# GpSimd's subtractions on VectorE, and a margin behind the data for background matmuls

## Chip, cores and metric

The kernel runs on one core of a Trainium2 chip. The metric is the device time of one execution in microseconds; before the change three runs gave a median of 1106.71 (1105.04 to 1108.61).

## What is computed

Two request groups of 512 positions by 1024 channels go through the same two encoder layers and a final norm, in float32:

```python
def encoder_layer(x, c, g_norm, w_ada, b_ada, w_in, w_out, decay_fwd, decay_bwd):
    ...
    mod = jax.nn.silu(c) @ w_ada + b_ada
    shift, scale, gate = jnp.split(mod, 3, axis=-1)
    h = rmsnorm(x, g_norm) * (1.0 + scale[:, None, :]) + shift[:, None, :]
    proj = h @ w_in
    qa, ka, va, ga, qb, kb, vb, gb = jnp.split(proj, idx, axis=-1)
    ...
    ya = oa.reshape(B, S, A_WIDTH) * jax.nn.silu(ga)
    ...
    r = yf + yb
    r = r * lax.rsqrt(jnp.mean(r * r, axis=-1, keepdims=True) + EPS)
    yr = r.astype(x.dtype).reshape(B, S, R_WIDTH) * jax.nn.silu(gb)
    out = jnp.concatenate([ya, yr], axis=-1) @ w_out
    return x + gate[:, None, :] * out
```

Mixer A is window attention with rotary query and key in three dilations, merged by their softmax denominators; mixer B is retention in both directions with a norm for each head.

## The kernel before

**High and low halves.** Float32 products are made of three matmuls on rounded operands: high by high, high by low and low by high. The high half is a rounding copy (ScalarE), the low half the difference between the value and its high half. So each operand costs one conversion and one subtraction. The input weights come in 56 tiles of 128x1024 (`raw`, made into `wH` and `wL` by `prepper`, line 797), the output weights in 16 (`rawo` into two `wo`, `prep_o`, line 830). The hidden state of layer 0 comes in eight tiles of 128x512 for each input (`hT`, `first_affine`, line 728), the mixed outputs as `yT` (`splitter`, line 1182). GpSimd does three of the subtractions: all `wL`, the second `wo`, and the low `hT` of the second input in layer 0. VectorE does the rest.

**Stages.** For each layer the kernel walks through a list of items: projections of query and key pairs of the window attention ("p"), of retention ("r"), their values ("v", "w") and gates ("g"), each for input 0 and then input 1. An item of one weight tile is 24 matmuls for each input. Rotary tables, attention scores, softmax, transposes by DMA, value products, retention products and norms of the items that are done run as background work between the matmuls of later items. After the items comes the output projection (`wo` by `yT`), then the residual and the norm of the next layer. At the start the modulation products (`wa` by `siluT`) come in pieces as their weights land; the projection matmuls of the first items for input 0 lie between them, and then the second input's hidden tiles are made: a transpose on TensorE, a copy and a conversion on ScalarE, a scaling on VectorE (`xT`) and the subtraction.

**The retention norm.** `r_out` (line 1135) adds up the squares of four heads on TensorE (four matmuls 32x512 by `small`), takes the inverse root on VectorE in place (`rsqrt`, line 484: two integer operations and three rounds of three), writes the rows `nwr` and broadcasts them with four matmuls by `selg`. It happens twice in a layer.

**What sets the order.** The instructions are written out by a planner while the program is built. `Plan` (line 128 on) keeps a planned time at which each engine is free and each tile is ready; `note` moves it on by a table of costs for each operation. Background steps are generators that yield a condition, the planned time from which they may be issued. Before each main matmul `pump` (line 220) issues every background step whose time is not behind TensorE's planned time; where the main matmul itself isn't ready, it issues the earliest one. Once written, the order is fixed; on the chip an instruction starts when its semaphores allow it. Two functions give the times: `at` (the tiles' planned time plus LAT, 200 ns) for steps that go to TensorE or to a transfer, and `after(engine, ...)` for steps of another engine, which is zero as soon as the tiles are ready before that engine is free. For VectorE and GpSimd the planner also keeps a list of times at which one holds the other off (`port`, `held`).

All engine calls go through one helper, so every row of the profile names line 391; the tiles tell what it is.

Of the kernel before, what the change touches and what calls it, by code (L numbers as in the profile page):

```python
# [47 lines left out]
AHEAD = 3000.0  # L48
LAT = 200.0
SAME = {"DVE": 127.0}  # L50
NMAIN = 5
# [73 lines left out]
class Plan:  # L125


    def __init__(self):
        self.free = {"PE": 0.0, "DVE": 0.0, "ACT": 0.0, "POOL": 0.0, "SP": 0.0}
        self.dma = 0.0  # L130
        self.port = {"DVE": [], "POOL": []}
        self.ready = {}
        self.last = {}
        self.slots = {}
        self.dead = set()
        self.tasks = []

    def keys(self, a):
# [21 lines left out]
    def held(self, eng, start, cost):  # L160

        other = self.port["POOL" if eng == "DVE" else "DVE"]
        for s, e in other:
            if s < start + cost and e > start:
                start = e
        own = self.port[eng]
        own.append((start, start + cost))
        del own[:-64]
        return start

    def note(self, eng, cost, outs, ins, nbytes=0.0, port=False):
# [209 lines left out]
class Engine:  # L381
# [5 lines left out]
    def __getattr__(self, op):  # L387
        fn = getattr(self.eng, op)

        def call(*args, **kw):  # L390
# [10 lines left out]
            if self.name == "SP":  # L401
                nbytes = outs[0].free_size() * outs[0].shape[0] * (2.0 / 290.0 if outs[0].dtype == F16 else 4.0 / 360.0)
            psum = any(a.tensor.name.startswith("banks") for a in ins)
            port = self.name == "POOL" or (self.name == "DVE" and not psum)
            self.plan.note(self.name, self.cost(op, outs, ins), outs, ins, nbytes, port)
            return r
        return call

    def cost(self, op, outs, ins):
# [26 lines left out]
        if self.name == "POOL":  # L436
            return 30.0 + 2.37 * n
        if op == "dma_start_transpose":
# [5 lines left out]
def trunk_kernel(  # L444
# [8 lines left out]
    plan = Plan()  # L453
    V, A, G, T, Q = (Engine(plan, n, e) for n, e in (("DVE", nc.vector), ("ACT", nc.scalar), ("POOL", nc.gpsimd),
                                                     ("PE", nc.tensor), ("SP", nc.sync)))
    cp = ctx.enter_context(tc.tile_pool(name="cp", bufs=1))
# [131 lines left out]
    def first_mod(ks):  # L588
        nk = len(ks)
        yield lambda: H.avail(2, 2 * nk, 8)  # L590
        w = first_load(ks)
        yield lambda: max(plan.at(bias, siluT, *w[0:2]), B.avail())
        bk = B.take()
# [7 lines left out]
        for k in range(KT):  # L601
            if k == 4 and nk == 2:
                yield lambda: plan.at(*w[2:4])
            for n in range(2 * nk):
# [8 lines left out]
        B.free(bk)  # L613
        yield lambda: max(plan.at(m), B.avail())
        cb = B.take()
# [112 lines left out]
    def first_affine(b, k, bk, xT):  # L728
# [3 lines left out]
        else:  # L732
            A.activation(xT, bk, AF.Copy)
        B.free(bk)
        yield lambda: (max(plan.after("ACT", xT), plan.after("DVE", xT), plan.at(acol, scol), H.avail(1, 2, 4, "R"))
                       if ("cols", 0, k) in have else INF)
# [11 lines left out]
    def prep_h(l, b):  # L748
        keys = [(l, b, t) for t in range(TT)]
        for k in range(KT):  # L750
            yield lambda: (max(plan.at(*(xh[x] for x in keys)), plan.at(acol, scol), B.avail(), H.avail(1, 2, hold[0], "R", 1))
                           if ("cols", l) in have and all(x in xh for x in keys) else INF)
# [44 lines left out]
    def prepper():  # L797
        for job in jobs:
            wts[job] = []
            for t in range(ntiles(*job[1:])):  # L800
# [29 lines left out]
    def prep_o(l):  # L830
        for k in KORDER:
# [26 lines left out]
    def main_wide(pj, job, l, b):  # L858
        for t in range(TT):
            out = pj[:, t // 2, (t % 2) * 256:(t % 2) * 256 + 256]  # L860
            for k in range(KT):
                pump(lambda: (max(plan.at(*wts[job][k // 4][2:]), plan.at(*hT[(l, b, k)]))
                              if (l, b, k) in hT and len(wts.get(job, ())) > k // 4 else INF))
# [8 lines left out]
    def rope(pj, c, s, res, b):  # L872
# [18 lines left out]
        for i, x in enumerate((*hi, *lo)):  # L891
            yield lambda: plan.at(x) - 700.0
            Q.dma_start(rd[:, i % 2, i // 2, :], x)
        H.free(*c, *s)
        yield lambda: max(plan.at(rd) - 500.0, H.avail(1, 6, K_STK, "R"))
        out = []
# [63 lines left out]
    def soften(p, b, ih, h, sS, tn, res):  # L960
# [22 lines left out]
        for t in pts[1:]:  # L983
            yield lambda: max(plan.at(t), W_T.avail())
            pT = W_T.take(1, "pT")
# [56 lines left out]
    def value(p, pj, res):  # L1042
# [13 lines left out]
        B_IN.free(pj)  # L1056
        yield lambda: max(plan.at(vt), W_T.avail())
        vn = W_T.take(1, "vn")
# [188 lines left out]
    def store(dst, src):  # L1247
        yield lambda: plan.at(src)
        Q.dma_start(split(dst, 2), src)
# [27 lines left out]
    for l in range(DEPTH):  # L1277
# [77 lines left out]
        for b in range(NB):  # L1355
            for t in range(TT):
# [8 lines left out]
                for c, (n0, n1) in enumerate(LAST if final else ((0, D),)):  # L1365
                    for n, k in enumerate(KORDER):
                        pump(lambda: plan.at(*yT[(k, b)], *wo[k]) if (k, b) in yT and k in wo else INF)
                        y, w = ([x.bitcast(F32R) for x in z] for z in (yT[(k, b)], wo[k]))
# [48 lines left out]
```

## Time and profile before

| | before |
|---|---|
| median of three runs | 1106.71 us |
| the profiled execution | 1106.17 us |
| its span, first to last instruction | 1104.0 us |
| TensorE busy | 1052.3 us |
| VectorE busy | 774.1 us |
| ScalarE busy | 467.8 us |
| GpSimd busy | 194.7 us |
| mean granted clock of TensorE | 0.987 |

TensorE's busy time covers a matmul until its modelled end, so what can be read from it is mainly where it has none. The granted clock (PEclk) is 1.00 at 2.4 GHz and 0.50 at 1.2 GHz; a stretch with 0.91 spent part of its time at the lower level. An idle time in brackets behind a row stands in front of that instruction, and the name behind the arrow is what ended it.

### The profile page before, as it was taken

To read this page: it belongs to the slowest core of one execution; us is meant where nothing else is said; L and a number is where in the kernel's file an instruction comes from. 1 tells how busy PE (TensorE), PEld (TensorE's weight loads), DVE (VectorE), ACT (ScalarE), POOL (GpSimd) and SP (SyncE) were. 2 spreads that over 40 slices of the span, in tenths; PEclk is the share of its full clock that TensorE was granted. 3 is DMA by queue.
4 is the path that set the end of the run, shared out by engine and by line. 5 is a ranking of instruction groups with operands and counts; after the bars stand their busy time and mean duration, and the time that the engine had idled before them with its cause. 6 is when DMAs were issued, how large, how long until landed. Compare 5 with 4: busy or idle time off the path is not lost.

```text
span 1104.0 us, 14884 instructions
## 1 busy us (share of the span) xinstructions
PE 1052.3 (95%) x5443; PEld 832.7 (75%) x5443; DVE 774.1 (70%) x1536; ACT 467.8 (42%) x808; POOL 194.7 (18%) x84
## 2 busy tenths in 40 slices
PE   5989999989999899989999999989999899999997
PEld 3758578877688777767888778867798777778886
DVE  5686655598565988767447885589766987757555
ACT  6455413418234266572233552426434257534101
POOL 3152010120101111181000111112101111143000
PEclk9989999999999999989999999999999999999999
DMA  9826995069970599964221697048851599942232
GB/s 314 310 64 185 272 311 180 5 231 233 299 245 20 173 227 268 219 163 152 77 86 68 229 182 237 20 134 205 188 165 44 186 227 263 211 115 96 77 115 77
DMA packets 217337, 189.64 MB, mean 172 GB/s; under 512 B 156656, under 2 KB 167184, under 8 KB 217264
## 3 DMA queue, kind: packets, MB, share of 16 engines
q1 hardware_dynamic: 217264, 188.69, 60.5%
q8 instruction: 43, 0.70, 0.3%
q14 instruction: 30, 0.25, 0.1%
HBM read 117.34 MB, written 33.57 MB: 137 GB/s over the span
## 4 chain that ended last, share of the span: by engine, by line
PE 73%; DVE 13%; DMA 3%; SPq 2%; issue 2%; ACT 1%; POOL 1%; DVEq 0%; POOLq 0%; ACTq 0%
PE banks L391 73%; DVE yr L391 2%; DVE rsq L391 2%; SPq L391 2%; DVE th L391 1%; DVE hT L391 1%; DVE sd L391 1%; DMA KL<-stk_dram 1%; DVE pt L391 1%; DVE rc L391 1%; DMA wa<-in_w_ada_dram 1%; DVE xT L391 1%; DMA pT<-pt 1%; DMA raw<-in_w_in_dram 0%; DMA KS<-stk_dram 0%
## 5 line engine op out<-in xcount | busy, mean ns | idle before, releaser
L391 PE MATMUL banks<-hT,wH 128*128 128x512 f32 x1536 | 484.0, 396 | 6.7 <-POOL hT L391 4.4
L391 PEld LDWEIGHTS banks<-hT,wH 128*128 128x128 f32 x1536 | 288.4, 190 | 83.7 <-issue 14.8
L391 PE MATMUL banks<-hT,wL 128*128 128x512 f32 x768 | 301.3, 392 | 0.0
L391 POOL TENSOR_TENSOR wL<-raw,wH 128x1024 fp32r<-128x1024 f32 x56 | 141.2, 2529 | 724.6 <-ACT wH L391 635.1
L391 PE MATMUL banks<-wo,yT 128*128 128x512 f32 (+1 forms) x792 | 179.5, 388 | 5.1 <-DVE yT L391 2.8
L391 PEld LDWEIGHTS banks<-wo,yT 128*128 128x128 f32 x792 | 146.5, 190 | 36.6 <-DVE yT L391 4.9
L391 PEld LDWEIGHTS banks<-hT,wL 128*128 128x128 f32 x768 | 145.6, 190 | 30.8
L391 PE MATMUL banks<-wH,hT 128*128 128x256 f32 x512 | 97.3, 284 | 0.0
L391 PEld LDWEIGHTS banks<-wH,hT 128*128 128x128 f32 x512 | 81.7, 191 | 4.0 <-issue 2.5
L391 ACT ACTIVATE wH<-raw 128x1024 fp32r<-128x1024 f32 x56 | 58.2, 1052 | 42.4 <-DMA raw<-in_w_in_dram 30.6
L391 PE MATMUL banks<-wL,hT 128*128 128x256 f32 x256 | 72.4, 283 | 0.0
L391 ACT ACTIVATE sq<-xr 128x1024 bf16<-128x1024 f32 (+2 forms) x18 | 17.3, 963 | 114.8 <-DVE xr L391 71.0
L391 DVE SCALAR_TENSOR_TENSOR pt<-sS,sm,pt 128x512 f16<-128x512 f32 x65 | 60.9, 977 | 3.4 <-ACT pt L391 2.8
L391 ACT ACTIVATE sS<-sS,sm 128x512 f32<-128x512 f32 x65 | 46.2, 712 | 28.8 <-DVE sm L391 28.0
L391 DVE TENSOR_TENSOR res<-banks,gb 128x512 f32<-128x512 f32 (+1 forms) x33 | 22.1, 671 | 49.0 <-PE banks L391 49.0
L391 DVE CUSTOM_DVE_ANT_0 sS<-banks,tabs 128x512 f32<-128x512 f32 x65 | 42.3, 687 | 19.7 <-PE banks L391 19.6
L391 POOL TENSOR_TENSOR wo<-rawo,wo 128x1024 fp32r<-128x1024 f32 x16 | 41.2, 2595 | 49.2 <-ACT wo L391 25.4
L391 PEld LDWEIGHTS banks<-wL,hT 128*128 128x128 f32 x256 | 49.0, 191 | 1.0
L391 PE MATMUL banks<-sr,rv 128*128 128x512 f32 x169 | 47.0, 391 | 0.0
L391 PE MATMUL banks<-pT,vn 128*64 128x512 f16 x384 | 45.1, 381 | 1.3 <-DMA pT<-pt 1.3
L391 ACT ACTIVATE pt<-sS,sm 128x512 f16<-128x512 f32 x65 | 43.2, 710 | 5.6 <-DVE sm L391 3.3
L391 PE MATMUL banks<-wa,siluT 128*32 128x128 f32 (+1 forms) x384 | 33.8, 398 | 7.9 <-DMA wa<-in_w_ada_dram 7.9
(278 smaller groups left out, 1407.6 us busy)
## 6 DMA issues: line engine op xcount, KB each, us to landing
raw<-in_w_in_dram SPq DMA_DIRECT2D x56, 512.0 KB, 5.4
wa<-in_w_ada_dram SPq DMA_DIRECT2D x48, 512.0 KB, 6.6
QS<-stk_dram SPq DMA_DIRECT2D x48, 256.0 KB, 3.6
KS<-stk_dram SPq DMA_DIRECT2D x48, 256.0 KB, 4.5
KL<-stk_dram SPq DMA_DIRECT2D x44, 256.0 KB, 4.6
rawo<-in_w_out_dram SPq DMA_DIRECT2D x16, 512.0 KB, 4.6
stk_dram<-rs SPq DMA_DIRECT2D x28, 256.0 KB, 2.7
stk_dram<-sd SPq DMA_DIRECT2D x23, 256.0 KB, 2.5
```

The costliest lines, as they stand in the source:

```text
L391: r = fn(*args, **kw)
```

## The change

The subtractions of `wL`, `wo` and `hT` go to VectorE; GpSimd has no work left. In `prepper` and `prep_o` the subtraction becomes a step of its own that is issued when the high half is ready by the plan. The list of mutual holds and GpSimd's costs leave the planner. `at` no longer adds 200 ns for all tiles; it adds an amount by the engine that makes the tile (SLACK). A new function `soon` keeps the old 200 ns, and main matmuls, transfers and `after` use it; `at` stays with the background steps that go to TensorE: scores, value products, retention products, norms, modulation products and the transposes of hidden tiles.

```diff
+SLACK = {"PE": 200.0, "ACT": 400.0, "DVE": 900.0, "DMA": 1500.0}
...
+    def made(self, *tiles):
+        return [self.ready[k] for t in tiles for k in self.keys(t) if k in self.ready]
+
     def at(self, *tiles):
-        return max((self.ready.get(k, (0.0, ""))[0] for t in tiles for k in self.keys(t)), default=0.0) + LAT
+
+        return max((t + SLACK[eng] for t, eng in self.made(*tiles)), default=0.0)
+
+    def soon(self, *tiles):
+        return max((t for t, _ in self.made(*tiles)), default=0.0) + LAT
 
     def after(self, eng, *tiles):
-        t = self.at(*tiles)
+        t = self.soon(*tiles)
         return 0.0 if t <= self.free[eng] else t
...
-        if port:
-            start = self.held(eng, start, cost)
...
-        (V if b == 0 else G).tensor_tensor(h[1].bitcast(F32R), xT, h[0], op=ALU.subtract)
+        V.tensor_tensor(h[1].bitcast(F32R), xT, h[0], op=ALU.subtract)
...
-                G.tensor_tensor(lo, raw, h.bitcast(F32), op=ALU.subtract)
+                yield lambda: plan.after("DVE", w[0])
+                V.tensor_tensor(lo, raw, h.bitcast(F32), op=ALU.subtract)
...
-                    G.tensor_tensor(t.bitcast(F32R), raw, out[0], op=ALU.subtract)
+                    yield lambda: plan.after("DVE", out[0])
+                    V.tensor_tensor(t.bitcast(F32R), raw, out[0], op=ALU.subtract)
...
     def main_half(out, job, t, l, b, ks=range(KT)):
         for k in ks:
-            pump(lambda: (max(plan.at(wts[job][t][2], wts[job][t][3]), plan.at(*hT[(l, b, k)]))
+            pump(lambda: (plan.soon(*wts[job][t][2:], *hT[(l, b, k)])
```

The order of the instructions moves nearly everywhere, since each issue time depends on those before. Three places, all on VectorE, show what the prediction speaks of.

The second input's hidden tiles in layer 0, from the last step of the decays (`ldec`) on; `xT` (once `th`) is scaled in place, and `hT` is its low half. Before:

```order
L391 TENSOR_SCALAR ldec<-ldec 128x8
L391 TENSOR_SCALAR xT<-xT,acol,scol 128x512 x3
L391 SCALAR_TENSOR_TENSOR th<-th,banks 128x512
L391 TENSOR_SCALAR xT<-xT,acol,scol 128x512
L391 TENSOR_SCALAR th<-th,acol,scol 128x512
L391 TENSOR_SCALAR xT<-xT,acol,scol 128x512
L391 TENSOR_TENSOR xT<-banks,tabs 128x512
```

Now:

```order
L385 TENSOR_SCALAR ldec<-ldec 128x8
L385 TENSOR_SCALAR xT<-xT,acol,scol 128x512
L385 TENSOR_TENSOR hT<-xT,hT 128x512
L385 TENSOR_SCALAR xT<-xT,acol,scol 128x512
L385 TENSOR_TENSOR hT<-xT,hT 128x512
L385 TENSOR_SCALAR xT<-xT,acol,scol 128x512
L385 TENSOR_TENSOR hT<-xT,hT 128x512
```

Each scaling is now followed by its subtraction, eight pairs in all, and the first rotary product (`banks,tabs`) comes behind the last of them, where it came before the last two scalings.

The first retention norm, around the copy of the sums of squares out of PSUM (`TENSOR_SCALAR ...<-banks`) that begins the chain to `nwr`. Before:

```order
L391 TENSOR_TENSOR sd<-sd,rs 128x512
L391 TENSOR_SCALAR rsq<-banks 128x512
L391 TENSOR_TENSOR rsq<-rsq,rs 128x512
L391 TENSOR_TENSOR sd<-sd,rs 128x512
L391 TENSOR_SCALAR yr<-rsq 128x512
L391 TENSOR_SCALAR yr<-yr 128x512
L391 TENSOR_TENSOR yr<-yr 128x512
```

Now:

```order
L385 TENSOR_TENSOR sr<-rs,KL 128x512
L385 TENSOR_TENSOR wL<-raw,wH 128x1024
L385 TENSOR_SCALAR yr<-banks 128x512
L385 TENSOR_SCALAR nw_1989<-yr 128x512
L385 TENSOR_SCALAR sS<-nw_1989 128x512
L385 TENSOR_TENSOR nw_1989<-sS 128x512
```

A wL subtraction now stands in front of the copy, and the two rotary operations that stood between the copy and the integer operations are gone from there. On TensorE 57 projection matmuls stand between the sums and the broadcast of `nwr` before, at all four norms; now it is 51, 54, 51 and, at the last, 69 with 4 background matmuls among them.

The end of layer 0, where the output projection's operands are made; `wo` are output weights, `yT` the low halves of the mixed outputs. Before:

```order
L391 TENSOR_TENSOR y<-y,yr 128x512
L391 SCALAR_TENSOR_TENSOR yr<-yr,banks 128x512
L391 TENSOR_TENSOR sd<-sd,yr 128x512
L391 SCALAR_TENSOR_TENSOR yr<-yr,banks 128x512
L391 TENSOR_TENSOR yr<-yr 128x512
L391 TENSOR_TENSOR yT<-th,yT 128x512
L391 TENSOR_TENSOR yT<-sS,yT 128x512
```

Now:

```order
L385 TENSOR_TENSOR th<-th,yr 128x512
L385 TENSOR_TENSOR wo<-rawo,wo 128x1024 x3
L385 TENSOR_TENSOR yT<-th,yT 128x512 x2
L385 TENSOR_TENSOR yT<-yr,yT 128x512
L385 TENSOR_TENSOR yT<-th,yT 128x512
L385 TENSOR_TENSOR yT<-yr,yT 128x512
L385 SCALAR_TENSOR_TENSOR th<-th,banks 128x512
L385 TENSOR_TENSOR yT<-th,yT 128x512
```

Five `yT` now stand ahead of the last gate's product (`th<-th,banks`), which all of them followed before, and three `wo` stand ahead of them. On ScalarE six conversions to `yT` stand ahead of the last gate's tanh, where all sixteen stood behind it. On TensorE the last value product of layer 0 (24 matmuls of `pT` by `vn`) stood 9 matmuls ahead of the output projection and now stands behind its first 30.

## Rows read from the trace of the kernel before

**Rows 1.** The page: busy us, share of the span, instructions by engine.
```profile
PE 1052.3 (95%) x5443; PEld 832.7 (75%) x5443; DVE 774.1 (70%) x1536; ACT 467.8 (42%) x808; POOL 194.7 (18%) x84
```

**Rows 2.** Busy time by stretch; columns as in the first line below.
```profile
core 0: us, PE busy (x) PEld busy (x) DVE busy (x) ACT busy (x) POOL busy (x), PEclk, DMA share, GB/s
60.00:80.00 20.00, 15.56 (x69) 10.95 (x68) 17.74 (x40) 12.41 (x21) 12.67 (x9) 0.90 0.14 51
80.00:100.00 20.00, 20.00 (x82) 15.90 (x82) 9.23 (x26) 9.30 (x22) 4.34 (x2) 0.93 0.59 187
...
120.00:140.00 20.00, 18.58 (x102) 10.12 (x94) 15.72 (x40) 11.88 (x25) 0.00 (x0) 1.00 1.05 289
220.00:240.00 20.00, 16.77 (x67) 13.10 (x66) 19.49 (x26) 4.15 (x6) 5.09 (x2) 0.91 0.60 196
360.00:380.00 20.00, 17.05 (x76) 13.77 (x75) 19.52 (x26) 3.42 (x5) 5.24 (x2) 1.00 0.60 196
480.00:500.00 20.00, 15.49 (x64) 9.60 (x62) 14.03 (x8) 13.40 (x21) 20.00 (x8) 0.83 0.44 159
720.00:760.00 40.00, 37.06 (x159) 28.97 (x158) 36.06 (x68) 16.48 (x32) 5.97 (x3) 0.96 0.50 163
860.00:880.00 20.00, 16.82 (x74) 13.28 (x73) 19.59 (x35) 3.72 (x9) 1.05 (x1) 1.00 0.47 158
920.00:940.00 20.00, 18.29 (x84) 13.41 (x83) 14.01 (x40) 14.56 (x29) 2.38 (x1) 0.91 1.11 261
1020.00:1040.00 20.00, 20.00 (x90) 16.57 (x89) 10.86 (x30) 2.30 (x4) 0.00 (x0) 1.00 0.23 80
```

**Rows 3.** Timeline at the first norm: start us, us, engine, operation; VectorE, GpSimd, TensorE.
```profile
220.18 0.69 DVE L391 TENSOR_SCALAR rsq<-banks 128x512 f32<-128x512 f32 x1
...
221.99 0.42 DVE L391 TENSOR_SCALAR yr<-rsq 128x512 int32<-128x512 int32 x1
222.44 2.50 DVE L391 TENSOR_SCALAR yr<-yr 128x512 int32<-128x512 int32 x1
...
226.43 0.69 DVE L391 SCALAR_TENSOR_TENSOR yr<-yr 128x512 f32<-128x512 f32 x1
...
228.61 2.82 DVE L391 SCALAR_TENSOR_TENSOR yr<-yr 128x512 f32<-128x512 f32 x1
...
234.50 0.75 DVE L391 SCALAR_TENSOR_TENSOR nwr<-nwr,small,rsq 128x512 fp32r<-128x512 f32 x1
...
221.96 2.70 POOL L391 TENSOR_TENSOR wL<-raw,wH 128x1024 fp32r<-128x1024 f32 x1 [21.49 <-ACT wH L391]
228.49 2.39 POOL L391 TENSOR_TENSOR wL<-raw,wH 128x1024 fp32r<-128x1024 f32 x1 [3.83 <-ACT wH L391]
...
235.30 0.96 PE L391 MATMUL banks<-nwr,selg 128*128 128x512 f32 x3 [2.99 <-DVE nwr L391]
```

**Rows 4.** Timeline where the second input's hidden tiles are made: TensorE, VectorE, GpSimd.
```profile
57.78 0.50 PE L391 MATMUL banks<-hT,wH 128*128 128x512 f32 x1 [0.55 <-DVE hT L391]
...
58.35 1.94 PE L391 MATMUL banks<-small,x 128*128 128x128 f32 x16
...
77.28 0.80 PE L391 MATMUL banks<-hT,wH 128*128 128x512 f32 x1 [2.96 <-POOL hT L391]
...
80.69 1.05 PE L391 MATMUL banks<-hT,wH 128*128 128x512 f32 x2
...
57.64 0.54 DVE L391 TENSOR_SCALAR xT<-xT,acol,scol 128x512 f32<-128x512 f32 x1
...
64.18 2.43 DVE L391 TENSOR_SCALAR xT<-xT,acol,scol 128x512 f32<-128x512 f32 x3
...
64.87 5.77 POOL L391 TENSOR_TENSOR hT<-xT,hT 128x512 fp32r<-128x512 f32 x4 [33.81 <-DVE xT L391]
```

**Rows 5.** Timeline at the end of layer 0, VectorE: a first and a later yT.
```profile
489.31 2.86 DVE L391 TENSOR_TENSOR yT<-th,yT 128x512 fp32r<-128x512 f32 x1
...
500.48 0.68 DVE L391 TENSOR_TENSOR yT<-yr,yT 128x512 fp32r<-128x512 f32 x1
```

**Rows 6.** Groups of instructions: count, busy us, mean ns, idle before.
```profile
L391 DVE TENSOR_TENSOR rv<-banks,rv 128x1024 fp32r<-128x1024 f32 x8 | 9.8, 1225 | 42.0 <-ACT rv L391 42.0
```

More of the change, by code (lines that the diff above doesn't have):

```diff
@@ L128, in __init__ @@
     def __init__(self):
-        self.free = {"PE": 0.0, "DVE": 0.0, "ACT": 0.0, "POOL": 0.0, "SP": 0.0}
+        self.free = {"PE": 0.0, "DVE": 0.0, "ACT": 0.0, "SP": 0.0}
         self.dma = 0.0
-        self.port = {"DVE": [], "POOL": []}
         self.ready = {}
@@ L151, in keys, with note @@
         return [slot + (u,) for u in sorted(units)]
+    def made(self, *tiles):
+        return [self.ready[k] for t in tiles for k in self.keys(t) if k in self.ready]
     def at(self, *tiles):
-        return max((self.ready.get(k, (0.0, ""))[0] for t in tiles for k in self.keys(t)), default=0.0) + LAT
+        return max((t + SLACK[eng] for t, eng in self.made(*tiles)), default=0.0)
+    def soon(self, *tiles):
+        return max((t for t, _ in self.made(*tiles)), default=0.0) + LAT
     def after(self, eng, *tiles):
-        t = self.at(*tiles)
+        t = self.soon(*tiles)
         return 0.0 if t <= self.free[eng] else t
[L160 to L171, printed above, removed]
+    def note(self, eng, cost, outs, ins, nbytes=0.0):
         part = eng == "SP" and (outs[0].shape[0] < P or outs[0].tensor.name.startswith("stk"))
@@ L402, in call @@
                 nbytes = outs[0].free_size() * outs[0].shape[0] * (2.0 / 290.0 if outs[0].dtype == F16 else 4.0 / 360.0)
-            psum = any(a.tensor.name.startswith("banks") for a in ins)
-            port = self.name == "POOL" or (self.name == "DVE" and not psum)
-            self.plan.note(self.name, self.cost(op, outs, ins), outs, ins, nbytes, port)
+            self.plan.note(self.name, self.cost(op, outs, ins), outs, ins, nbytes)
             return r
@@ L435, in cost @@
             return (53.0 if psum else 93.0) + 93.0 * extra + 0.833 * n
-        if self.name == "POOL":
-            return 30.0 + 2.37 * n
         if op == "dma_start_transpose":
@@ L453, in trunk_kernel @@
     plan = Plan()
-    V, A, G, T, Q = (Engine(plan, n, e) for n, e in (("DVE", nc.vector), ("ACT", nc.scalar), ("POOL", nc.gpsimd),
-                                                     ("PE", nc.tensor), ("SP", nc.sync)))
+    V, A, T, Q = (Engine(plan, n, e) for n, e in (("DVE", nc.vector), ("ACT", nc.scalar), ("PE", nc.tensor),
+                                                  ("SP", nc.sync)))
     cp = ctx.enter_context(tc.tile_pool(name="cp", bufs=1))
@@ L591, in first_mod @@
         w = first_load(ks)
-        yield lambda: max(plan.at(bias, siluT, *w[0:2]), B.avail())
+        yield lambda: max(plan.soon(bias, siluT, *w[0:2]), B.avail())
         bk = B.take()
@@ L602, in first_mod @@
             if k == 4 and nk == 2:
-                yield lambda: plan.at(*w[2:4])
+                yield lambda: plan.soon(*w[2:4])
             for n in range(2 * nk):
@@ L613, in first_mod @@
         B.free(bk)
-        yield lambda: max(plan.at(m), B.avail())
+        yield lambda: max(plan.soon(m), B.avail())
         cb = B.take()
@@ L734, in first_affine @@
         B.free(bk)
-        yield lambda: (max(plan.after("ACT", xT), plan.after("DVE", xT), plan.at(acol, scol), H.avail(1, 2, 4, "R"))
+        yield lambda: (max(plan.after("ACT", xT), plan.after("DVE", xT), plan.soon(acol, scol), H.avail(1, 2, 4, "R"))
                        if ("cols", 0, k) in have else INF)
@@ L750, in prep_h @@
         for k in range(KT):
-            yield lambda: (max(plan.at(*(xh[x] for x in keys)), plan.at(acol, scol), B.avail(), H.avail(1, 2, hold[0], "R", 1))
+            yield lambda: (max(plan.at(*(xh[x] for x in keys)), plan.soon(acol, scol), B.avail(), H.avail(1, 2, hold[0], "R", 1))
                            if ("cols", l) in have and all(x in xh for x in keys) else INF)
@@ L861, in main_wide @@
             for k in range(KT):
-                pump(lambda: (max(plan.at(*wts[job][k // 4][2:]), plan.at(*hT[(l, b, k)]))
+                pump(lambda: (plan.soon(*wts[job][k // 4][2:], *hT[(l, b, k)])
                               if (l, b, k) in hT and len(wts.get(job, ())) > k // 4 else INF))
@@ L891, in rope @@
         for i, x in enumerate((*hi, *lo)):
-            yield lambda: plan.at(x) - 700.0
+            yield lambda: plan.soon(x) - 700.0
             Q.dma_start(rd[:, i % 2, i // 2, :], x)
         H.free(*c, *s)
-        yield lambda: max(plan.at(rd) - 500.0, H.avail(1, 6, K_STK, "R"))
+        yield lambda: max(plan.soon(rd) - 500.0, H.avail(1, 6, K_STK, "R"))
         out = []
@@ L983, in soften @@
         for t in pts[1:]:
-            yield lambda: max(plan.at(t), W_T.avail())
+            yield lambda: max(plan.soon(t), W_T.avail())
             pT = W_T.take(1, "pT")
@@ L1056, in value @@
         B_IN.free(pj)
-        yield lambda: max(plan.at(vt), W_T.avail())
+        yield lambda: max(plan.soon(vt), W_T.avail())
         vn = W_T.take(1, "vn")
@@ L1247, in store @@
     def store(dst, src):
-        yield lambda: plan.at(src)
+        yield lambda: plan.soon(src)
         Q.dma_start(split(dst, 2), src)
@@ L1366, in trunk_kernel @@
                     for n, k in enumerate(KORDER):
-                        pump(lambda: plan.at(*yT[(k, b)], *wo[k]) if (k, b) in yT and k in wo else INF)
+                        pump(lambda: plan.soon(*yT[(k, b)], *wo[k]) if (k, b) in yT and k in wo else INF)
                         y, w = ([x.bitcast(F32R) for x in z] for z in (yT[(k, b)], wo[k]))
```

## The prediction

> **What bounds the kernel now.** I read the busy shares first, then the table of 20-us stretches, then single instructions in the stretches where TensorE idles. The shares [rows 1] give TensorE 1052.3 of 1104.0 us: it is the bound, and no matmul is added or removed, so only its 51.7 us without work and the time at a lower clock can go. The stretches [rows 2] are to be read for two things: 20.00 minus PE's busy time, and PEclk under 1.00. A stretch without trouble is 1020 to 1040: 90 matmuls of 512 columns in 20.00 us, 0.222 us each. Idle time, and 20 us times what PEclk lacks of 1, add up to four losses:
> 60 to 100 us: 4.44 idle, and 2.0 and 1.4 of clock, 7.8 us (the second input's hidden tiles);
> 220 to 240, 360 to 380, 720 to 760 and 860 to 880 (the retention norms): 3.23, 2.95, 2.94 and 3.18 idle, and 1.8 and 1.6 of clock at the first and the third, 15.7 us;
> 480 to 500 (end of layer 0): 4.51 idle and 3.4 of clock, 7.9 us;
> 120 to 140 and 920 to 940 (attention scores that wait for transfers): 1.42 and 1.71 idle, 1.8 of clock, 4.9 us.
> That is 36.3 us. The lower level is 1.2 GHz against 2.4, and here it shows only in stretches with idle time or right behind one. The rest of the idle time lies at the start (first transfers), behind the last matmul and in scattered pieces; I let it stand.
>
> **What VectorE waits for.** At the first norm [rows 3] two integer operations of one form follow each other: 0.42 us, then 2.50 us. The second runs from 222.44 to 224.94, GpSimd's subtraction from 221.96 to 224.66; a later operation takes 2.82 us against 0.69, from 228.61 to 231.43, beside GpSimd's 228.49 to 230.88. Both end just behind GpSimd's. So VectorE stands still while GpSimd works, and GpSimd's time is largely taken from VectorE.
>
> **The subtractions, moved.** They are 56 of wL and 16 of wo (128x1024) and 8 of hT (128x512). No row shows the large one on VectorE. Nearest are 1.225 us for the same operation with one input in PSUM [rows 6] and twice 0.68 us for half the width in SBUF [rows 5], 1.36. I take 1.23, nearer the same width: 72 x 1.23 + 8 x 0.68 = 94 us more on VectorE. What goes is between the two excesses of rows 3 (4.2 us) and all of GpSimd's 194.7 us; over the kernel VectorE ends between 774 - 101 and 774 + 90 us, at most 78% of the span. On the path that sets the end this counts only where TensorE waits for VectorE; so it is costed by place.
>
> *Start, 60 to 100 us.* The second input's eight hidden tiles are made as a scaling on VectorE and a subtraction on GpSimd, 5.77 us for four of these [rows 4], and TensorE waits up to 2.96 us for them. In the new order each subtraction follows its scaling on VectorE. From 64.18 us, where the scalings begin, eight pairs of 0.54 + 0.68 and one gate operation of about 0.7 end at 74.6, the first pair at 65.4. When does TensorE ask? Between the last modulation product, which waits for its transfer either way, and the transposes of the second input at 58.35 us stand 54 projection matmuls now and 60 in the new order: 1.3 us more, less the wait of 0.55 in front of 57.78. So it gets there at about 59.1; 30 matmuls (6.7 us) and 32 transposes (twice 1.94) bring it to 69.7, and from there it wants one pair every 0.67 us, the last at 74.4. A wait of some 0.2 us stays, and the 24 matmuls end near 75.2; today the next item begins at 80.69. That is 5.5 us, and 1.4 of low clock behind it; less the doubt about the five wL that now stand on VectorE ahead of the very first hidden tile, **6 us** (2 to 7.8).
>
> *Four retention norms.* VectorE's chain from the copy of the sums to the norm's rows goes from 220.18 to 235.25. Less the excess (2.08 + 2.13) and the two rotary operations inside it (from 220.18 to 221.99, less the copy's 0.69: 1.1) it is 9.8 us. TensorE now has 57 matmuls between the sums and the broadcast at each of the four; in the new order 51, 54, 51 and over 60. So the margin does not push the broadcast back; it comes up to 6 matmuls earlier, after 51 x 0.222 = 11.3 us, and still 1.5 us are left. Today's 12.7 us against 15.1 come short by 2.4; with handing over, the trace has 2.99 us of wait. A wL subtraction stands right in front of the copy: it is hidden by the nine matmuls ahead of the sums, and if its weights come late, 1.23 us eat most of the 1.5. All four waits go, and the low clock behind two of them: **15 us** (9 to 15.7).
>
> *End of layer 0.* Four of the yT subtractions take 2.86 us and more beside GpSimd, 0.68 us without it [rows 5]; that is 8.8 us of a chain on which the output projection stands. In the new order six of the first input's eight yT are converted ahead of the last gate's tanh, so before the projection asks, and three wo subtractions (3.7 us) stand in front of them on VectorE. Late next is the last wo, behind two wL: 30 projection matmuls, the last value product and 12 more cover it (some 12 us). **7.5 us** (3 to 7.9).
>
> *The margin.* It is no wait: it only decides whether a main matmul or a background one is put into TensorE's stream first. Behind a transfer it is 1500 ns in place of 200, behind VectorE 900. The two stretches idle 1.42 and 1.71 us; a score there now stands up to 1.3 us of main work further behind its transfer. Queued behind a late background matmul is all of TensorE's stream, so each avoided wait counts in full. **3.5 us** of 4.9 (0 to 4.9). Its price: the attention work slides back, at the end of layer 0 so far that the last value product stands behind 30 output matmuls, not in front. It is needed only by the second input, some 160 matmuls later, so I cost that at nothing.
>
> *Sum.* 6 + 15 + 7.5 + 3.5 = 32 us; new small waits take 1 (0 to 15; the nearest rows are the waits of 1 to 3 us above). The profiled execution's 1106.17 us (span 1104.0 and 2.2 around it) becomes 1075.2; the median of the runs is 0.5 above it, so 1075.7, rounded to **1075**.
>
> **Rivals.**
> VectorE becomes the bound (slower). Place: the stretches in which its row is full, 220 to 240, 360 to 380, 860 to 880, with 19.5 of 20 us. The weights' low halves then queue behind softmax and rope, and the third matmul of a tile waits. If each of some 48 tiles behind the start came one subtraction late, 48 x 1.23 = 59 us, less 32: 1134 us. It decides from 0.67 us per tile on. Against it: the full stretches hold the blocked time itself, other stretches have VectorE idle, and no wait of TensorE in the trace names wL. Chance 0.06. The Trainium skill, "Perfetto Trace Analysis", section on optimizing Scalar and DVE operations, says that with a saturated DVE handing work to GPSIMD may make sense, which speaks against this change and would give this rival's time; the same place says that offloading between these two might not help because they share a read port. Rows 3 bear out the second half.
> The waits are handed on. Later attention work and fuller queues bring new waits of half the gain: 1091 us. For it: this kind of plan has left 36 us of such losses already. Chance 0.17.
> It does not do what it says: the slow VectorE operations are slow in themselves. Then the norms' chain keeps its 4.2 us, 14.0 against 11.3, so 2.7 us of wait stay at each and the gain there shrinks to 2; the end of layer 0 gains nothing, and 94 us are truly added. Start 4, norms 2, margin 3.5: 1097 us. Against it: one form, 0.42 and 2.50 us, next to each other. Chance 0.05.
> Gains and new waits cancel: 1106 us, chance 0.04.
>
> **How the numbers follow.** The forecast has 0.68. The range reaches from all of the 36.3 us and some scattered idle time (1064) to the handed-on case (1092); that leaves out somewhat under 2 in 10. Under about 0.3% this kernel's runs can't be told apart. Faster: 0.68 + 0.17 + 0.05 = 0.90; within 0.3%: 0.04; slower: 0.06.
>
> **What would show it.** Right: no VectorE operation of 128x512 above about 1.5 us; no TensorE wait for nwr above 1 us; PEclk 1.00 behind the first norm and at the end of layer 0; VectorE's busy time within 60 us of 774. Wrong: TensorE waiting for VectorE's wL or wo, 128x1024 subtractions well above 1.4 us, or waits at the value products and scores where none stood.

## The result, and the profile after

| | before | after |
|---|---|---|
| median of the runs made side by side | 1105.88 us (1104.37 to 1108.61) | 1070.16 us (1069.01 to 1071.55) |
| the profiled execution, and its span | 1106.17, 1104.0 | 1071.55, 1069.8 |
| TensorE without work in the span | 51.7 us | 28.2 us |
| VectorE busy | 774.1 us | 776.4 us |
| GpSimd busy | 194.7 us | 0.2 us |

The ratio is 0.9675, 95% interval 0.9651 to 0.9698: faster by 35.7 us. Forecast were 1075 us and a range of 1064 to 1092. The profiled execution of after is 1.4 us above its median; its mean granted clock is 0.994, that of the other three 0.998 to 0.999.

The page of after, the line that answers to [rows 1]:

```profile
PE 1041.6 (97%) x5443; PEld 832.8 (78%) x5443; DVE 776.4 (73%) x1616; ACT 467.0 (44%) x807; POOL 0.2 (0%) x4
```

VectorE has 80 instructions more and is busy 2.3 us longer. What the 80 cost is in the groups of instructions of after (count, busy us, mean ns, idle time in front):

```profile
L385 DVE TENSOR_TENSOR wL<-raw,wH 128x1024 fp32r<-128x1024 f32 x56 | 67.9, 1220 | 13.3 <-ACT wH L385 13.2
L385 DVE SCALAR_TENSOR_TENSOR pt<-sS,sm,pt 128x512 f16<-128x512 f32 x88 | 61.8, 746 | 3.7 <-ACT pt L385 3.6
L385 DVE TENSOR_TENSOR wo<-rawo,wo 128x1024 fp32r<-128x1024 f32 x16 | 19.2, 1221 | 3.8 <-ACT wo L385 3.8
```

That is 67.9 + 19.2, and 5.5 for the eight hT at 0.69: 92.6 us of work, for which 90 us elsewhere went away.

The stretches of after, to be held against [rows 2] (columns as there; the stretches lie a little differently in the program, since the kernel is shorter). Below them are two of before that [rows 2] did not have:

```profile
20.00:40.00 20.00, 16.93 (x190) 12.40 (x189) 12.64 (x24) 6.00 (x7) 0.00 (x0) 0.83 1.09 357
60.00:80.00 20.00, 19.71 (x101) 15.53 (x100) 18.73 (x56) 14.01 (x24) 0.00 (x0) 1.00 0.01 2
80.00:100.00 20.00, 20.00 (x88) 16.10 (x87) 17.75 (x32) 7.47 (x14) 0.00 (x0) 1.00 0.62 203
120.00:140.00 20.00, 20.00 (x105) 14.59 (x103) 12.29 (x22) 6.19 (x13) 0.00 (x0) 1.00 1.09 242
160.00:180.00 20.00, 18.26 (x121) 12.80 (x120) 11.63 (x16) 5.21 (x7) 0.00 (x0) 1.00 0.93 299
220.00:240.00 20.00, 20.00 (x93) 15.59 (x92) 15.43 (x25) 3.87 (x6) 0.00 (x0) 1.00 0.48 164
360.00:380.00 20.00, 20.00 (x90) 16.55 (x89) 19.45 (x33) 3.33 (x4) 0.00 (x0) 1.00 0.53 183
480.00:500.00 20.00, 20.00 (x101) 15.35 (x100) 15.69 (x28) 8.52 (x11) 0.00 (x0) 1.00 0.67 247
860.00:880.00 20.00, 20.00 (x90) 16.58 (x89) 19.75 (x52) 16.94 (x37) 0.00 (x0) 1.00 0.50 116
920.00:940.00 20.00, 20.00 (x101) 15.31 (x101) 16.86 (x48) 16.52 (x37) 0.00 (x0) 1.00 0.53 111
```

```profile
0.00:20.00 20.00, 7.30 (x55) 5.27 (x55) 9.65 (x54) 11.89 (x16) 2.46 (x5) 1.00 0.93 291
20.00:40.00 20.00, 18.56 (x231) 12.81 (x229) 13.71 (x25) 6.74 (x8) 9.82 (x5) 1.00 1.09 357
```

The second number is TensorE's busy time: 20.00 where [rows 2] had 15.5 to 18.6. Two of these stretches are worse than before: the start, 16.93 at a clock of 0.83 from 20 to 40 us, where before had 18.56 at 1.00, and 160 to 180 us, 18.26 where before had 20.00; there TensorE waits 0.5 us for transposed softmax rows and 1.2 for modulation weights. Idle time and low clock by place, from the same tables with all stretches:

| place | lost before | lost after | gain | term of the prediction |
|---|---|---|---|---|
| 0 to 60 us | 14.7 | 15.9, and 3.4 of clock | -4.6 | in the 6 below |
| 60 to 100 | 7.8 | 0.3 | 7.5 | 6 |
| four retention norms | 15.7 | 0.0 | 15.7 | 15 |
| end of layer 0 | 7.9 | 0.0 | 7.9 | 7.5 |
| 120 to 140, 920 to 940 | 4.9 | 0.0 | 4.9 | 3.5 |
| all else up to the last matmul | 4.7 | 4.0 | 0.7 | -1 |
| sum | | | 32.1 | 31 |

The spans differ by 34.2; 2.1 us show in no gap. The first norm of after, to be held against [rows 3] (start in us, duration, engine, operation):

```profile
225.87 0.69 DVE L385 TENSOR_SCALAR yr<-banks 128x512 f32<-128x512 f32 x1 [4.06 <-PE banks L385]
226.60 0.43 DVE L385 TENSOR_SCALAR nw<-yr 128x512 int32<-128x512 int32 x1
227.06 0.43 DVE L385 TENSOR_SCALAR sS<-nw 128x512 int32<-128x512 int32 x1
...
234.92 0.75 DVE L385 SCALAR_TENSOR_TENSOR nwr<-nwr,small,yr 128x512 fp32r<-128x512 f32 x1
...
237.41 1.10 PE L385 MATMUL banks<-nwr,selg 128*128 128x512 f32 x4
```

Both integer operations take 0.43 us. The chain lasts from 225.87 to 235.67, 9.8 us, and the broadcast starts 1.7 us behind its end with no idle time in front.

### The profile page after: what moved, and what is told of

The parts are those of the page before. It is cut to its first block, busy times and chain, and to the rows that moved or that the text cites. A ratio compares the mean times of both kernels' runs of the same rounds, so it can differ in the third digit from the quotient of the medians.

```text
span 1069.8 us, 14718 instructions
## 1 busy us (share of the span) xinstructions
PE 1041.6 (97%) x5443; PEld 832.8 (78%) x5443; DVE 776.4 (73%) x1616; ACT 467.0 (44%) x807; POOL 0.2 (0%) x4
## 4 chain that ended last, share of the span: by engine, by line
PE 83%; DMA 6%; DVE 5%; SPq 3%; ACT 2%; issue 2%; DVEq 0%; ACTq 0%
PE banks L385 83%; DMA wa<-in_w_ada_dram 3%; SPq L385 3%; DMA pT<-pt 1%; DMA stk_dram<-rc 1%; DVE nst L385 1%; DMA KL<-stk_dram 1%; ACT pt L385 1%; DVE sS L385 1%; ACT sS L385 1%; DVE dt L385 1%; DVE xT L385 0%; DVE hT L385 0%; DVE rsq L385 0%; DMA stk_dram<-b 0%
## 5 line engine op out<-in xcount | busy, mean ns | idle before, releaser
L385 PE MATMUL banks<-hT,wH 128*128 128x512 f32 x1536 | 478.7, 393 | 2.9 <-DVE hT L385 2.8
L385 PE MATMUL banks<-wo,yT 128*128 128x512 f32 (+1 forms) x792 | 176.2, 384 | 0.0
L385 DVE TENSOR_TENSOR wL<-raw,wH 128x1024 fp32r<-128x1024 f32 x56 | 67.9, 1220 | 13.3 <-ACT wH L385 13.2
L385 ACT ACTIVATE sS<-sS,sm 128x512 f32<-128x512 f32 x88 | 62.6, 713 | 19.0 <-DVE sm L385 18.6
L385 DVE CUSTOM_DVE_ANT_0 sS<-banks,tabs 128x512 f32<-128x512 f32 x88 | 57.1, 686 | 9.3 <-PE banks L385 9.3
L385 ACT ACTIVATE pt<-sS,sm 128x512 f16<-128x512 f32 x88 | 58.7, 710 | 11.7 <-DVE sm L385 7.2
L385 ACT ACTIVATE sq<-xr 128x1024 bf16<-128x1024 f32 (+2 forms) x15 | 14.2, 944 | 92.9 <-DVE xr L385 44.3
L385 PEld LDWEIGHTS <-vn 128*64 128x64 f16 x384 | 21.9, 110 | 21.7 <-issue 6.4
```

The lines of the kernel that those rows point to most:

```text
L385: r = fn(*args, **kw)
```

## The experiments

Ratios are against the kernel before, timed on the same chip; its median was 1105.7 to 1106.5 us beside these runs and 1105.9 beside after, so differences between times of separate runs are good to about 1 us. The first two keep an order word for word and change only the engine that executes the subtractions, so nothing but the engine differs. All others change the order too, from the first difference to the end of the kernel.

**Old order, VectorE executes.**

```diff
 in before:
-    V, A, G, T, Q = ... ("POOL", nc.gpsimd), ...
+    V, A, G, T, Q = ... ("POOL", nc.vector), ...
```

> The kernel before with its instruction order left as it was on every engine's side (TensorE, ScalarE and the transfers keep their order word for word); only the 80 subtractions of GpSimd are executed by VectorE, at the place where the program issues them. The planner still believes in GpSimd. Theory (VectorE stood still while GpSimd worked): the 128x512 operations at the norms take 0.4 to 0.8 us, the four norm waits go (15 us), the end of layer 0 gives about 7, the second input's hidden tiles about 4, the two stretches with late transfers keep their 4.9: 1080 us (1074 to 1088), VectorE's busy time within 20 us of 774. Rival 'the new order brings the gain': nothing that the order set is changed, so 1100 us or more, with the norm waits in place. Rival 'slow in themselves': the slow operations stay above 2 us, VectorE's busy time rises by 94 us, 1097 us or more.

Measured: 1108.48 us, ratio 1.0009 (0.9995 to 1.0023), no change. The theory had 1080. Yet the blocking is gone. The page of this run, its softmax rows (pt), the same group in before, and the stretches of this run:

```profile
PE 1051.7 (95%) x5443; PEld 832.6 (75%) x5443; DVE 777.6 (70%) x1616; ACT 468.0 (42%) x808; POOL 0.2 (0%) x4
L391 DVE SCALAR_TENSOR_TENSOR pt<-sS,sm,pt 128x512 f16<-128x512 f32 x65 | 45.9, 747 | 3.9 <-ACT pt L391 2.6
```

```profile
L391 DVE SCALAR_TENSOR_TENSOR pt<-sS,sm,pt 128x512 f16<-128x512 f32 x65 | 60.9, 977 | 3.4 <-ACT pt L391 2.8
```

```profile
220.00:240.00 20.00, 19.59 (x89) 15.19 (x88) 19.42 (x31) 5.49 (x7) 0.00 (x0) 1.00 0.63 210
360.00:380.00 20.00, 19.97 (x87) 15.96 (x87) 19.52 (x33) 2.56 (x5) 0.00 (x0) 1.00 0.62 201
480.00:500.00 20.00, 14.82 (x61) 9.96 (x60) 16.36 (x23) 14.33 (x23) 0.00 (x0) 0.74 0.53 190
760.00:780.00 20.00, 15.38 (x62) 12.36 (x60) 18.15 (x45) 13.16 (x27) 0.00 (x0) 0.91 0.86 162
860.00:880.00 20.00, 19.59 (x87) 15.73 (x86) 19.52 (x33) 2.63 (x5) 0.00 (x0) 1.00 0.61 201
```

The norms have 19.6 to 20.0 where [rows 2] had 16.8 to 17.1: some 14 us are won there, clock included. They are lost again elsewhere: 480 to 500 loses 10.4 us (7.9 in before), 760 to 780 loses 6.4 (0.7 in before), the first 40 us 3.5 more than in before, 420 to 440 another 1.8. The place at 760, from idle VectorE to waiting TensorE:

```profile
757.64 1.04 ACT L391 ACTIVATE wH<-raw 128x1024 fp32r<-128x1024 f32 x1
...
758.72 1.23 DVE L391 TENSOR_TENSOR wL<-raw,wH 128x1024 fp32r<-128x1024 f32 x1 [4.92 <-ACT wH L391]
759.86 1.22 DVE L391 TENSOR_REDUCE vs<-banks 128x1 f32<-128x1024 f32 x1
...
764.14 0.69 DVE L391 CUSTOM_DVE_ANT_0 sd<-banks,tabs 128x512 f32<-128x512 f32 x1
...
764.89 0.73 PE L391 MATMUL banks<-hT,wH 128*128 128x512 f32 x2 [4.62 <-DVE sm L391]
```

VectorE stood idle 4.92 us in front of a subtraction whose high half ScalarE had not made yet. Behind it in the same queue stood work that empties PSUM banks (`vs<-banks`, `sd<-banks`), and TensorE stopped at 760.3 for 4.62 us until, by the names, that was done. Over the kernel VectorE idles 55.2 us in front of wL, against 13.3 in after:

```profile
L391 DVE TENSOR_TENSOR wL<-raw,wH 128x1024 fp32r<-128x1024 f32 x56 | 67.8, 1222 | 55.2 <-ACT wH L391 55.2
```

So a new cause came up that the prediction lacked: on GpSimd an early subtraction waited alone, on VectorE everything behind it waits too. Followed to TensorE it is at 760 alone, 6.4 us of the loss. From 480 to 500 us VectorE likewise idles 3.01 us in front of a wL, and TensorE then waits 2.82 us for a yT that stands behind it; for the first 40 us and 420 to 440 the cause is not shown.

**New order, GpSimd executes.**

```diff
 in after:
-                V.tensor_tensor(lo, raw, h.bitcast(F32), op=ALU.subtract)
+                G.tensor_tensor(lo, raw, h.bitcast(F32), op=ALU.subtract)
...
-                    V.tensor_tensor(t.bitcast(F32R), raw, out[0], op=ALU.subtract)
+                    G.tensor_tensor(t.bitcast(F32R), raw, out[0], op=ALU.subtract)
 (and the low hT of the second input; the planner still counts all three to VectorE)
```

> The changed kernel with its order kept (TensorE's word for word), but the same 80 subtractions executed by GpSimd. Theory (blocking): 128x512 operations on VectorE of 2.4 to 2.9 us come back beside GpSimd's, the waits for nwr, for the hidden tiles and for yT come back; what the margin and the new order gained stays. 1070 + 15 + 7 + 3 = 1095 us (1085 to 1112), VectorE's busy time again about 774. Rival 'the new order brings the gain': 1070 to 1080 us.

Measured: 1090.75 us, 0.9849 (0.9825 to 0.9873), 20.6 us above after; inside the theory's range, outside the rival's. The operations that stand still are back, here, below the page of this run, at the first norm and at the end of layer 0:

```profile
PE 1046.3 (96%) x5443; PEld 829.2 (76%) x5443; DVE 775.3 (71%) x1536; ACT 466.6 (43%) x807; POOL 193.2 (18%) x84
...
229.67 2.40 POOL L385 TENSOR_TENSOR wL<-raw,wH 128x1024 fp32r<-128x1024 f32 x1 [3.43 <-ACT wH L385]
229.76 2.59 DVE L385 TENSOR_SCALAR nw<-yr 128x512 int32<-128x512 int32 x1
232.39 0.43 DVE L385 TENSOR_SCALAR sS<-nw 128x512 int32<-128x512 int32 x1
...
487.37 2.87 DVE L385 TENSOR_TENSOR yT<-th,yT 128x512 fp32r<-128x512 f32 x1
487.50 1.65 PE L385 MATMUL banks<-wo,yT 128*128 128x512 f32 x6 [1.12 <-DVE yT L385]
```

The norm's chain takes 12 us here, against 9.8 in after and 15.1 in before. Only one GpSimd subtraction falls into it, and TensorE waits 0.55 us, not 3; at the other three norms it waits 0.47, 1.00 and 0.73. That is 2.75 us left of the norms' 15.7, and in the old order with VectorE it was 1.5: either change by itself takes most of these waits away. At the end of layer 0 four waits of about 1.1 us in front of yT came back. That GpSimd needs about 2.5 us for a subtraction, and VectorE 1.22, can be seen in few waits: only 1.5 us of TensorE's waits end with one of GpSimd's (hT), none with a wL or wo. Idle time and low clock up to the last matmul are 12.0 us more than in after (35.7 and 23.7), where the profiled spans differ by 18.3; the other 6 us show in no gap.

Together: moving the engine is worth nothing in the old order, 20.6 us in the new one; the new order is worth 15.4 us with GpSimd, 38 with VectorE.

**The subtraction no longer a step of its own.**

```diff
 in after:
-                yield lambda: plan.after("DVE", w[0])
                 V.tensor_tensor(lo, raw, h.bitcast(F32), op=ALU.subtract)
...
-                    yield lambda: plan.after("DVE", out[0])
                     V.tensor_tensor(t.bitcast(F32R), raw, out[0], op=ALU.subtract)
```

> The changed kernel with one thing undone: the subtractions of wL and wo on VectorE are again issued right behind their conversion, not as a step of their own that waits until the high half is ready by the plan. Theory (head of the queue: with the order of before, VectorE idled 55 us in front of wL, whose high half wasn't there yet, and all that was queued behind it was late; the step of its own takes that away): VectorE's idle time in front of wL and wo grows from 17 to 45 us or more, part of it lands on TensorE: 1080 us (1075 to 1090). Rival 'it is enough that the planner counts the subtraction to VectorE': the time stays at 1070 to 1073 us.

Measured: 1088.87 us, 0.9844 (0.9814 to 0.9874). The idle time in front of wL and wo is 48.0 and 8.8 us, where after has 13.3 and 3.8. Most of the loss is one chain, read here from the idle VectorE through the transfer to TensorE:

```profile
470.60 1.23 DVE L385 TENSOR_TENSOR wo<-rawo,wo 128x1024 fp32r<-128x1024 f32 x1 [6.01 <-ACT wo L385]
471.74 0.74 DVE L385 SCALAR_TENSOR_TENSOR pt<-y,sm,pt 128x512 f16<-128x512 f32 x1
471.85 12.01 SPq L385 DMA_TRANSPOSE pT<-pt  x4
...
483.93 1.06 PE L385 MATMUL banks<-pT,vn 128*64 128x512 f16 x4 [16.69 <-DMA pT<-pt]
```

Softmax rows (pt) stood behind a wo that was not ready for 6.01 us; their transposes went out late, and a value product that had been put into TensorE's stream for an earlier time held it 16.69 us. VectorE's idle time is 6 of these; the row of the four transposes itself spans 12.01. That the planner counts the subtraction to VectorE is therefore not enough; the step of its own keeps VectorE from that, by its idle time (17.1 us in front of wL and wo, 56.8 without the step). The size of the loss, though, is that of this one order (see below).

**The margin: undone, alone, halves of it, doubled.**

```diff
 in after, one at a time:
-SLACK = {"PE": 200.0, "ACT": 400.0, "DVE": 900.0, "DMA": 1500.0}
+SLACK = {"PE": 200.0, "ACT": 200.0, "DVE": 200.0, "DMA": 200.0}     # undone
+SLACK = {"PE": 200.0, "ACT": 200.0, "DVE": 200.0, "DMA": 1500.0}    # transfers alone
+SLACK = {"PE": 200.0, "ACT": 400.0, "DVE": 900.0, "DMA": 200.0}     # engines alone
+SLACK = {"PE": 400.0, "ACT": 800.0, "DVE": 1800.0, "DMA": 3000.0}   # doubled
 margin alone: SLACK as in after with "POOL": 900.0, subtractions, holds and costs of GpSimd as in before
```

> The changed kernel with the margin undone: 200 ns for every engine, the subtractions stay on VectorE. Theory (the margin is the 3.5 us of the prediction, at the stretches with late transfers): 1073.5 us (1071 to 1077), with waits of TensorE for transfers of K and of the transposed softmax rows of some 3 us in sum back. Rival 'the margin does most of it': 1085 us or more, since background steps that follow VectorE stall TensorE everywhere. Rival 'the margin does nothing': within 1 us of the changed kernel.

> The changed kernel with the move undone: the margin of the change (and the same 900 ns behind GpSimd), the subtractions on GpSimd and the planner's mutual holds and costs as before. Theory (blocking, margin small): 1102 us (1097 to 1108): norms and the end of layer 0 as before, the stretches with late transfers better by 3.5. Rival 'the margin does most of it': under 1090 us, with the norm waits gone although GpSimd still works.

> The changed kernel with the margin behind transfers alone (1500 ns); behind every engine 200. Theory (margin is worth 11 us, most of it where background steps stood behind transfers of the softmax rows, of K and Q and of the modulation weights): 1072 us (1069 to 1075), TensorE's waits for pT and KL under 2 us in sum. Rival 'the margin behind VectorE carries it': 1077 to 1081 us.

> The changed kernel with the margin behind the engines alone (ScalarE 400, VectorE 900 ns), behind transfers 200. Theory (the transfers' margin carries it): 1078 us (1075 to 1082), waits for pT of 4 to 6 us stay. Rival 'the margin behind VectorE carries it': 1070 to 1073 us.

> The changed kernel with all four margins doubled (400, 800, 1800, 3000 ns). Theory: the waits that the margin can take away are nearly all gone by now (TensorE's waits for transfers behind the start come to under 3 us), so at most 2 us are to be had, and softmax and norms slide back further: 1069 us (1067 to 1075). Rival 'later background work costs': 1076 us or more.

Measured: undone 1081.15 us, 0.9761 (0.9742 to 0.9780); alone with GpSimd 1104.21, 0.9984 (0.9970 to 0.9998); transfers alone 1081.10, 0.9779 (0.9753 to 0.9805); engines alone 1096.67, 0.9910 (0.9880 to 0.9940); doubled 1076.37, 0.9732 (0.9709 to 0.9756). Only the margin alone lies in the range of its theory; the other four lie above theirs, and doubled meets its rival. The two halves bring 0 and lose 15 us, both together win 11: no sum of causes gives that. What the rows show in each is single waits for the transposed softmax rows, at other places each time (doubled also waits 4.9 us for hidden tiles, after 2.8). TensorE's waits for pT, by run (total, times, longest; after has 0.8 in 2):

engines alone:

```profile
PE banks L385 <- DMA pT<-pt: 13.3, 6, 5.2
```

transfers alone:

```profile
PE banks L385 <- DMA pT<-pt: 7.0, 5, 2.6
```

doubled:

```profile
PE banks L385 <- DMA pT<-pt: 4.3, 3, 2.0
```

With the margin alone and GpSimd at work TensorE still waits 4.5 us for nwr, and 4.4 for the second input's hT.

**One order is a draw.** By this theory a small shift of any constant gives a new order, and with it a time as if drawn by lot. If that is so, margins next to those of the change must scatter as well.

```diff
 in after, one at a time:
-SLACK = {"PE": 200.0, "ACT": 400.0, "DVE": 900.0, "DMA": 1500.0}
+SLACK = {"PE": 180.0, "ACT": 360.0, "DVE": 810.0, "DMA": 1350.0}
+SLACK = {"PE": 220.0, "ACT": 440.0, "DVE": 990.0, "DMA": 1650.0}
+SLACK = {"PE": 250.0, "ACT": 250.0, "DVE": 250.0, "DMA": 250.0}
```

> The changed kernel with all four margins a tenth smaller (180, 360, 810, 1350 ns). No cause calls for a step between these and the margins of the change, so this measures how far the time of one plan stands for its margins. Theory 'one order is a draw': each small shift rearranges the order from there on, and where a value product or a modulation product happens to stand in front of a late transfer changes; the time lies 3 to 10 us above the changed kernel, with other single waits for pT or wa: 1076 us (1071 to 1082). Rival 'the margin itself is worth 11 us': 1069 to 1072 us, with waits for transfers as few as in the changed kernel.

> The changed kernel with all four margins a tenth larger (220, 440, 990, 1650 ns). Theory 'one order is a draw': 1076 us (1071 to 1082), with other single waits than at a tenth less. Rival 'the margin itself is worth 11 us': 1069 to 1072 us.

> The changed kernel without a margin worth the name: 250 ns behind every engine (200 gave 1081 us). Theory 'one order is a draw': the time differs from 1081 us by several us in either direction, 1083 us (1075 to 1095); if the draws without a margin lie above those with one, the margin does shift the mean. Rival 'the margin itself is worth 11 us and the order is no lottery': 1080 to 1082 us.

Measured: a tenth less 1073.55 us, 0.9693 (0.9666 to 0.9719); a tenth more 1088.51, 0.9817 (0.9788 to 0.9846), above the range expected; 250 ns for all 1091.52, 0.9844 (0.9813 to 0.9874), 10 us above 200 ns for all. A tenth of a margin moves the time by 18 us. At a tenth more, TensorE waits 7.4 us for pT in two waits and 3.2 for a retention operand, where after has 0.8 and none; at 250 ns it waits 8.0 us for yT and 6.7 for pT. Waits for nwr above 1 us are in none of the three.

**The start mended.** After loses 2.8 us in front of its first hidden tile:

```profile
26.97 2.34 DVE L385 TENSOR_TENSOR wL<-raw,wH 128x1024 fp32r<-128x1024 f32 x2
...
29.24 0.53 DVE L385 TENSOR_SCALAR dt<-dt,acol,scol 128x512 f32<-128x512 f32 x1
29.80 0.69 DVE L385 TENSOR_TENSOR hT<-dt,hT 128x512 fp32r<-128x512 f32 x1
...
30.55 0.80 PE L385 MATMUL banks<-hT,wH 128*128 128x512 f32 x1 [2.56 <-DVE hT L385]
```

```diff
 in after:
+    def first(job, t):
+        n = sum(ntiles(*j[1:]) for j in jobs[:jobs.index(job)]) + t
+        return n < 3 or n >= 8 or (0, 0, 0) in hT
...
-                yield lambda: plan.after("DVE", w[0])
+                yield lambda: plan.after("DVE", w[0]) if first(job, t) else INF
```

> The changed kernel with the start mended: of the first eight wL the fourth and later ones are not issued on VectorE before the first hidden tile's scaling and subtraction, which stood behind the two wL that end at 29.3 us in the changed kernel. The margins stay. Theory (the doubt of the prediction about the five wL): the wait of 2.8 us for the first hidden tile shrinks to under 1, TensorE's clock in the stretch from 20 to 40 us is 1.00 in place of 0.83; that is 2 to 5 us, behind which the order differs, by some us in either direction: 1068 us (1063 to 1078). Rival 'the third matmul of a tile waits for wL then': the same wait, now for wL, 1070 us or more.

Measured: 1106.35 us, 0.9996 (0.9980 to 1.0012). At its place it did what it should, and the rest of the order was the worst of all draws:

```profile
20.00:40.00 20.00, 18.64 (x241) 13.50 (x241) 15.14 (x32) 7.17 (x9) 0.00 (x0) 1.00 1.09 358
...
60.00:80.00 20.00, 15.71 (x78) 12.01 (x77) 18.87 (x51) 13.15 (x22) 0.00 (x0) 0.97 0.14 41
480.00:500.00 20.00, 12.09 (x48) 6.99 (x46) 17.09 (x30) 18.07 (x31) 0.00 (x0) 0.74 0.80 189
500.00:520.00 20.00, 14.86 (x66) 10.36 (x67) 14.21 (x19) 8.47 (x14) 0.00 (x0) 0.83 0.65 152
```

20 to 40 us is 1.7 us fuller and at full clock. But 60 to 80 us, 19.71 in after, is down to 15.71: TensorE waits 4.07 us for a hidden tile of the second input, where before idled 4.4 us. The margin runs with VectorE have the same pattern: with doubled margins 20 to 40 us idles 0.1 us and 60 to 80 4.7, in all the others it is 3.1 to 3.7 and at most 0.3. Whether an order without both waits exists is not shown. From 480 to 520 us 13.1 us are idle and 8.6 more lost to the clock, in front of value products whose transposes come late and of yT; in after that part of the program has none of it. No version here beats after.

## Why the prediction was right, and where it was not

*VectorE stands still while GpSimd works.* Right, and the two pairs with one order measure it. After has 92.6 us more work on VectorE than the same order with GpSimd and is busy 1.1 us longer (776.4 and 775.3), so 91.5 of GpSimd's 193.2 us were taken from VectorE; the pair in the old order gives 88.9. That is just under half, not "largely". The prediction had only 4.2 and 194.7 as bounds. The subtraction, 1.23 forecast, takes 1.22 us.

*Slow in themselves.* This rival is out: in one and the same order pt (65 of them) takes 977 ns beside GpSimd and 747 without.

*Norms.* 15 forecast, 15.7 measured; the chain of 9.8 us came out as worked out, the 1.5 us of cover as 1.7. The attribution was too simple: in this order the waits shrink to between 0.5 and 1.0 us with GpSimd too.

*End of layer 0.* 7.5 forecast, 7.9 measured; with GpSimd in the same order 4.5 us of waits for yT come back.

*Start.* The term that was mis-sized. 5.5 and 1.4 us were worked out for 60 to 100 us and 7.5 measured. For the five wL ahead of the first hidden tile 0.9 was taken off; they cost 1.6 us of idle time from 20 to 40 us, and 3.4 of low clock in the profiled execution. What is left of the 6 is 2.9, in the profiled execution; the median is 1.4 us faster, and the other three executions have the higher clock. The gain at 60 to 100 and the loss at 20 to 40 also belong together: where a run mended the second, it lost most of the first again.

*Margin.* At the two places named, 4.9 of 4.9 were won, 3.5 forecast. That this is the margin's work isn't shown: TensorE's waits for K and Q come to 3.0 us in before and 0.7 in after, but without the margin also to 0.5 (undone) and 0.5 (250 ns), and to 3.1 with the engines alone. What does go with the margin behind transfers is another wait: from 120 to 140 us the three orders with 200 or 250 ns idle 1.5 to 2.2 us in front of modulation products, the others that keep the work on VectorE and have 1350 or more 0 to 0.7. Undoing the margin costs 11 us, but 250 in place of 200 ns costs another 10, and a tenth more margin 18. With the move made and the start left alone, the four orders with all four margins gave 1070.2, 1073.6, 1076.4 and 1088.5 us, the four with less or part of them 1081.1, 1081.2, 1091.5 and 1096.7. The means are 1077.1 and 1087.6; with so few draws, so far apart, the margin's own worth stays open.

*New small waits, 1 us (0 to 15).* The step that carried more than the prediction knew. The sum was made for the four places that had lost time before, with the order of after in hand; what else that order might lose had no row to stand on. In after it is 0.7 less than before. The other draws lie up to 36 us above after, with waits mostly at value and modulation products whose transfers come late, in some for yT, a hidden tile or a retention operand. So the terms of the norms and of the end of layer 0 were right in size, and the pairs with one order show their mechanism, with what is said above on the norms; that the total came out at 1070 was luck. This order has the lowest time of the nine that move the work and keep the step of its own, whose mean is 1085 (the one at a tenth less can't be told from it: the intervals of the two ratios overlap). The rival "the waits are handed on" (1091) is what three of the nine did (1088 to 1097), and the rival "gains and new waits cancel" (1106) one.

*VectorE becomes the bound.* It did not: 19.45 and 19.75 of 20 us in two stretches of after, and TensorE full in both. The Trainium skill, "Perfetto Trace Analysis", section on optimizing Scalar and DVE operations, holds both halves of the matter; the half that offloading between these two engines might not help is the one the runs agree with, by 91.5 us given back for 92.6 taken.

*What the prediction missed in kind.* It costed the move by busy time and by chains. It did not ask what stands behind a subtraction whose input is late in VectorE's queue. The old order with VectorE lost all of the gain again, 6.4 us of it shown to be this price; the added step in `prepper` and `prep_o`, which the prediction did not cost, is what takes VectorE's idle time away. How many us of the total the step is worth stays open, since without it the order is another.

## What to carry to other kernels

Work that moves from a lightly used engine to a busy one also moves to another queue: look at what stands behind it there, and issue it only when its input is ready, or the wait that it had to itself becomes everybody's. To learn what an edit is worth where a planner writes the order, run the old engine in the new order and the new engine in the old one, and a few neighbours of the constants; a single order of this kernel stands for its idea only to some 10 us (the nine lie between 1070 and 1106).

## What the runs showed of the hardware

What GpSimd holds up depends on where VectorE's inputs are. Mean ns of one, in the same order with GpSimd working and then without (groups of instructions of the new order with GpSimd, then of after):

```profile
L385 DVE SCALAR_TENSOR_TENSOR pt<-sS,sm,pt 128x512 f16<-128x512 f32 x88 | 73.8, 883 | 3.5 <-ACT pt L385 3.3
L385 DVE CUSTOM_DVE_ANT_0 sS<-banks,tabs 128x512 f32<-128x512 f32 x88 | 57.2, 685 | 10.4 <-PE banks L385 10.4
```

```profile
L385 DVE CUSTOM_DVE_ANT_0 sS<-banks,tabs 128x512 f32<-128x512 f32 x88 | 57.1, 686 | 9.3 <-PE banks L385 9.3
```

pt, with two tiles in SBUF, goes from 746 to 883 ns; sS, with one of its two in PSUM, stays at 685. The integer operation of one input is held up too, 0.43 us and 2.59, though not each time: in [rows 3] the first of the two took 0.42, starting 0.03 us behind GpSimd's. The Trainium skill, "SBUF — State Buffer", section "Who interferes with whom", says that an instruction with two SBUF inputs contends with a GpSimd one that reads SBUF, and that `tensor_scalar` can enter modes in which it contends too; these numbers agree with it.

The time taken from VectorE, 91.5 us, is nearly what VectorE needs to do the subtractions itself, 92.6. That it comes out so even was not expected, and no run here says why.
